# Intermediate stores moved from SyncE's DMA queue to GpSimd's, and one Sqrt taken first of all

## The chip, the cores and the metric

The kernel runs on one core of a Trainium2 chip. The metric is the time of one execution on the device in microseconds (us). Five engines work side by side, each with an instruction stream of its own that it works through in order: TensorE (PE in the profile; its weight loads are PEld), VectorE (DVE), ScalarE (ACT), GpSimd (POOL) and SyncE (SP). Transfers between device memory and on-chip memory (SBUF) are issued by an engine as an instruction of its stream; where that instruction has to wait for its data or for a free buffer, everything behind it on this engine waits too.

## The reference, cut to what matters

One layer of a hybrid block on x of 1024 tokens by 2048 features: eight heads of neighbourhood attention and eight groups of a gated long convolution (Hyena) share one input projection, their results go through one output projection, and a mixture of 16 experts follows.

```python
h = rms_norm(x, mix_norm_g[i])
proj = jnp.einsum('bsd,de->bse', h, w_in[i])
q, k, v = jnp.split(proj[..., :3 * ATTN_WIDTH], 3, axis=-1)
...
attn = neighbourhood_attention(q, k, v, rpb[i])
filters = implicit_filters(s, filt_w1[i], filt_b1[i], filt_w2[i], filt_b2[i], filt_w3[i], filt_freq[i])
hy = hyena_mixer(proj[..., 3 * ATTN_WIDTH:], conv_w[i], conv_b[i], filters, filt_bias[i])
mixed = jnp.concatenate([group_rms_norm(attn, attn_out_g[i], N_ATTN_HEADS),
                         group_rms_norm(hy, hyena_out_g[i], N_HYENA_GROUPS)], axis=-1)
x = x + jnp.einsum('bsd,de->bse', mixed, w_out[i])
x = x + expert_choice_moe(rms_norm(x, ffn_norm_g[i]), w_router[i], w_gate[i], w_up[i], w_down[i])

def hyena_mixer(u, conv_w, conv_b, filters, filt_bias):
    u = short_conv(u, conv_w, conv_b)
    z = u[..., HYENA_ORDER * HYENA_WIDTH:]
    for o in range(HYENA_ORDER):
        gate = u[..., o * HYENA_WIDTH:(o + 1) * HYENA_WIDTH]
        z = gate * bidirectional_fft_conv(z, filters[:, o, 0], filters[:, o, 1], filt_bias[o])
    return z

def bidirectional_fft_conv(u, h_fwd, h_bwd, skip):
    taps = jnp.concatenate([h_fwd, jnp.zeros_like(h_fwd[:1]), h_bwd[:0:-1]], axis=0)
    spec = jnp.fft.rfft(uf, n=n, axis=1) * jnp.fft.rfft(taps, n=n, axis=0)[None]
    y = jnp.fft.irfft(spec, n=n, axis=1)[:, :length]
    return (y + uf * skip.astype(jnp.float32)).astype(u.dtype)
```

## The kernel before, in words

Each fp32 operand of a large product is split in two parts, high and low (`split`: ACT casts, DVE subtracts), and three products of the parts are added up. The stages are:

- **Start (0 to about 103 us).** `load_h` loads x in eight tiles of 128 tokens, sums squares on ACT (`sq`), takes the root (`st`), scales (`xs`), transposes and splits. The high part `hh` stays in SBUF, the low part goes to device memory (`lo_d`). The first input projection is done beside it.
- **Filters (about 103 to 812 us).** The input projection (`pj`) runs on as a stream that loads weights (`w`) and low parts (`hl`, five buffers, 608 loads) through SP's queue. Woven into it are six attention heads and 16 calls of `filt(u, o)`. Each `filt` makes two spectra `H` (i = 0, 1; one buffer, 128 by 1026) and stores each to `Hd` (32 stores of 513 KB).
- **Hyena (about 812 to 1640 us).** Eight groups. `hyena(u)` loads two spectra (`H<-Hd`) on SP and convolves through transforms written as matmuls.
- **Closing (about 1640 to 2140 us).** The last two attention heads (6 and 7), and the output projection (`o`) as a new stream: 56 loads `s<-sd` of 1 MB on SP into two buffers, and weights `b`.
- **Routing and experts (2140 to 3293 us).** Not touched.

The output projection is done by a Strassen-like scheme with seven products. For that `store_mixed` makes, for each of eight channel blocks, seven combinations of the mixed halves, splits each in a high and a low part (`mxh`, `mxl`, one buffer each), and stores both to one of the tensors `sd1` to `sd7` (112 stores of 256 KB; in the listings below `sd_60` is sd1, `sd_61` sd2, `sd_62` sd3, `sd_63` sd4, `sd_64` sd5, `sd_65` sd6, `sd_66` sd7). What the first of two visits to a channel block needs later goes to `half` (16 stores of 256 KB). Attention heads and Hyena groups share these buffers' pattern: `mxh` can be written again only when its store has landed.

The order of the work is set by `weave`: it lets the stream and the heads or groups take turns by a running estimate of PE's time. Each engine then gets its instructions in about that order, and the builder's own scheduler may move rows that don't depend on each other. Loads, stores and weights of the first stages all stand in SP's one stream. POOL has before the experts only small memsets (`T`, `pT`, `fz`, `raw`, `z`, `Z`) and 20 loads of constants: `m`, `amask`, `at_g`, `qkg`, `hy_u`, `hy_g` and others. ACT's first operation is `sq` (L173), its first root stands in L175.

The lines of the change: L143 (`self.eps`), L588 (store of `H`), L757 (stores of `mxh` and `mxl`), L772 (stores of `mx` and `mxo` to `half`). Loads that stand behind these on SP: L280 (`hl`), L266 (`w`), L691 (`H<-Hd`), L815 (`T`, the bias table of a head), L957 (`s<-sd`), L962 (`x`).

Of the kernel before, what the change touches and what calls it, by code (L numbers as in the profile page):

```python
# [7 lines left out]
F32 = mybir.dt.float32  # L8
# [3 lines left out]
AF = mybir.ActivationFunctionType  # L12
# [5 lines left out]
P = 128  # L18
# [19 lines left out]
class Block:  # L38
# [90 lines left out]
    def build(self, ctx):  # L129
        tc, nc, a = self.tc, self.nc, self.a  # L130
        self.dram = ctx.enter_context(tc.tile_pool(name="dram", bufs=1, space=DRAM))
        cst = ctx.enter_context(tc.tile_pool(name="cst", bufs=1))
        self.sd = {i: self.dram.tile([4, P, 2, NU, P], F32, name=f"sd{i}") for i in range(1, 8)}
        self.half = self.dram.tile([NU, 2, P, 512], F32, name="half")
        self.xg = self.dram.tile([S, D + 16], F32, name="xg")
        self.lo_d = self.dram.tile([KD, P, S], F32, name="lo_d")
        self.Hd = self.dram.tile([NU, 2, P, 2, NF], F32, name="Hd")
        self.ident = cst.tile([P, P], F32, name="ident")
        nc.scalar.dma_start(self.ident, a["c_ident"])
        eps = cst.tile([P, 16], F32, name="eps")  # L140
        nc.vector.memset(eps, EPS)
        self.eps = eps[:, 0:1]
        self.aff = cst.tile([P, NT // 2, 2, NE], F32, name="aff")  # L143
        self.gate = cst.tile([P, NE], F32, name="gate")
        self.idx = cst.tile([P, NE], I32, name="idx")
        self.outer = ctx
        with ExitStack() as self.tail:
            self.phase1()
            self.phase2()
        self.phase3(ctx)  # L150
# [387 lines left out]
    def filt(self, u, o):  # L538

        nc, a, pl, L = self.nc, self.a, self.fw, self.pace("filt")  # L540
        if o == 0:
            self.win = pl.tile([P, S], F32, name="win", bufs=1)
            nc.sync.dma_start(self.win, a["c_win"][u * P:(u + 1) * P, :])
        win = self.win
        w3 = pl.tile([P, 2, P], F32, name="w3", bufs=1)
        nc.sync.dma_start(w3, a["filt_w3"][u, o])
        yield 3.0
        ws = pl.tile([P, 512], F32, name="bt", bufs=1)[:, :2 * P].rearrange("p (i c) -> p i c", i=2)
        nc.vector.tensor_tensor(ws[:, 0], w3[:, 0], w3[:, 1], op=ALU.add)
        nc.vector.tensor_tensor(ws[:, 1], w3[:, 0], w3[:, 1], op=ALU.subtract)  # L550
        wr = pl.tile([P, 2, P], R, name="wr", bufs=2)
        nc.scalar.copy(wr, ws)
        nc.vector.tensor_tensor(wr[64:], ws[64:], wr[64:].bitcast(F32), op=ALU.subtract)
        p = self.ps("F")
        self.mm(p[:, :1], w3[:64, 0], self.hid_0, True, True)
        z0 = pl.tile([P, 1], F32, name="z0", bufs=2)
        nc.vector.scalar_tensor_tensor(z0, p[:, :1], win[:, 0:1], self.hy_s[:, u, o:o + 1],
                                       op0=ALU.mult, op1=ALU.add)
        yield L["td"]
        sc = 1.0 / 1024  # L560
        for i in range(2):
            z = pl.tile([P, S + 1], F32, name="fz", bufs=1)
            nc.gpsimd.memset(z[:, S:S + 1], 0.0)
            for s in range(2):
                sl = slice(s * 512, s * 512 + 512)
                p = self.ps("F")
                self.mm(p, wr[:, i], self.hid_h[:, sl], True, False)
                self.mm(p, wr[:, i], self.hid_l[:, sl], False, True)
                nc.vector.tensor_tensor(z[:, sl], p, win[:, sl], op=ALU.mult)
                yield L["fz"]  # L570
            nc.vector.tensor_copy(z[:, 0:1], z0)
            ze, zo = self.fold_o(pl, z)
            H = pl.tile([P, NF], F32, name="H", bufs=1)
            fl = self.sin_fold(pl, zo) if i else self.cos_fold(pl, ze)
            yield L["ff"] + 1.5
            hl = self.tsplit4(pl, fl, "FT")
            yield L["td"]
            if i:
                yield from self.sin_even(pl, H, hl, sc, "F", L)
            else:  # L580
                yield from self.cos_even(pl, H, hl, ze, sc, "F", L)
            z = ze[:, 0:512] if i else zo
            hl = self.tsplit4(pl, self.halves(z[:, 0::2]) + self.halves(z[:, 1::2]), "FT")
            yield L["td"]
            self.odd(pl, H, hl, sc, "F", i)
            if i == 0:
                nc.vector.tensor_scalar(H[:, 0:257:256], H[:, 0:257:256], 0.5, None, op0=ALU.mult)
            nc.sync.dma_start(self.Hd[u, o, :, i], H)  # L588
            yield L["dd"]
        yield L["fe"]  # L590

# [149 lines left out]
    def store_mixed(self, pool, u, src, g, role, L):  # L741

        nc = self.nc
        v, head = u % NU, u < NU
        second = head != (v < self.EARLY)
        m, p = [], []  # L750

        def store(i, x):
            hi = pool.tile([P, 512], R, name="mxh", bufs=1)
            lo = pool.tile([P, 512], R, name="mxl", bufs=1)
            self.split(hi, lo, x)
            for j, t in enumerate((hi, lo)):
                nc.sync.dma_start(self.sd[i][:, :, j, v, :].rearrange("t p c -> p t c"),  # L757
                                  t.bitcast(F32).rearrange("p (t c) -> p t c", t=4))

        for h in range(2):  # L760
            if second:
                p.append(pool.tile([P, 512], F32, name="mxp", bufs=2))
                nc.sync.dma_start(p[h], self.half[v, h])
            o = pool.tile([P, 4, P], F32, name="mxo", bufs=1)
            self.norm4(pool, o, src(h))
            yield L["mx"]
            pt = self.ps(role)
            self.flip(pt, [o[:, i] for i in range(4)])
            m.append(o.rearrange("p i c -> p (i c)") if h else pool.tile([P, 512], F32, name="mx", bufs=1))
            nc.scalar.activation(m[h], pt, AF.Copy, scale=g)  # L770
            if not second:
                nc.sync.dma_start(self.half[v, h], m[h])  # L772
            if h == 0 or not head:
                store((1 if head else 2) if h == 0 else 4, m[h])
            if h == 0:
                yield L["tt"]
        tt = nc.vector.tensor_tensor
        if second:
            yield L["tt"]
            tt(p[1], m[1], p[1], op=ALU.add)  # L780
            store(5, p[1])
        if head:
            yield L["tt"]
            tt(m[1], m[0], m[1], op=ALU.subtract)
            store(7, m[1])
        if second:
            yield L["tt"]
            a0, y0 = (m[0], p[0]) if head else (p[0], m[0])
            tt(a0, p[1], a0, op=ALU.subtract)
            store(6, a0)  # L790
            yield L["tt"]
            tt(y0, y0, a0, op=ALU.subtract)
            store(3, y0)
        self.mixed.add(u)
# [627 lines left out]
```

## Time and profile before

| what | value |
|---|---|
| median of 3 runs | 3293.3 us (3292.95 to 3294.88) |
| profiled execution: time, span | 3295.26 us, 3293.5 us |
| PE, DVE, ACT, POOL busy | 96%, 74%, 56%, 3% of the span |
| mean granted TensorE clock | 0.985 |
| SP's queue (q1), GpSimd's queue (q0) | 837.26 MB, 36.49 MB |
| chain that ended last | PE 83%, DMA 9%, DVE 3%, issue 3%, ACT 1% |

The span is the time from the first to the last instruction of the profiled execution; 1.8 us of the execution lie outside it. The chain that ended last is followed back from the last instruction, at each step to what released it. PE holds 83% of it, so a change off PE can only win where PE stands still or runs at its lower clock.

### The profile page before, as it was taken

The page shows a single profiled execution, that of the slowest core. Times are in us where ns is not written, and L with a number is a line of the kernel's source. Part 1 is how long each engine was busy: PE and PEld are TensorE (multiplying, and loading weights), DVE is VectorE, ACT ScalarE, POOL GpSimd, SP SyncE. Part 2 cuts the span into 40 slices and gives each one's busy share as a digit, 9 for nine tenths or more (in the row PEclk, how much of TensorE's full clock was granted, in tenths as well). Part 3 has the DMA queues.
Part 4 walks back from the last instruction along what each step waited for, and adds up shares of the span by engine and source line. Part 5 has one row for each costly group of instructions (what it writes and reads, how often), then busy time and mean ns, then how long its engine had stood idle before and what let it go on. Part 6 is the DMA issues. An engine that isn't in the chain of part 4 may idle for free.

```text
span 3293.5 us, 47095 instructions
## 1 busy us (share of the span) xinstructions
PE 3164.4 (96%) x17040; PEld 2756.7 (84%) x17040; DVE 2432.1 (74%) x3648; ACT 1851.8 (56%) x2881; POOL 85.1 (3%) x200
## 2 busy tenths in 40 slices
PE   8999999999999999999997999949999999999998
PEld 8899999998888888889986777738888888888887
DVE  5677776764567777677677455589989999899997
ACT  5455555543334344344353222548888888888886
POOL 0000000000000000000000000000000000000000
PEclk9999999999999999999998999979999999999999
DMA  7555555556676666665467886698999999999993
GB/s 250 192 166 171 178 188 191 166 180 207 198 223 203 202 218 210 223 208 193 156 224 253 288 282 209 224 365 343 403 398 391 405 404 404 392 398 405 403 404 133
DMA packets 311913, 876.82 MB, mean 266 GB/s; under 512 B 27108, under 2 KB 127631, under 8 KB 247936
## 3 DMA queue, kind: packets, MB, share of 16 engines
q1 hardware_dynamic: 305888, 837.26, 69.7%
q0 software_dynamic: 5648, 36.49, 4.3%
q8 instruction: 134, 2.20, 0.3%
q14 instruction: 99, 0.81, 0.1%
q10 hardware_dynamic: 144, 0.07, 0.0%
HBM read 781.07 MB, written 92.37 MB: 265 GB/s over the span
## 4 chain that ended last, share of the span: by engine, by line
PE 83%; DMA 9%; DVE 3%; issue 3%; ACT 1%; SPq 0%; POOLq 0%; POOL 0%; DVEq 0%; ACTq 0%
PE pa L68 30%; PE pj L68 29%; PE o L68 6%; PE c L68 5%; PE f L68 4%; DMA s<-sd 3%; PE a L68 3%; PE ct L79 2%; PE tp L1333 1%; DMA hl<-lo_d 1%; DMA sd<-mxl 1%; PE a L79 1%; PE ft L79 1%; DMA w<-in_w_down_dram 1%; PE t L79 1%
## 5 line engine op out<-in xcount | busy, mean ns | idle before, releaser
L60 ACT CAST wh<-w 128x1024 fp32r<-128x1024 f32 (+2 forms) x1180 | 990.2, 846 | 593.2 <-PE pj L68 369.8
L61 DVE TENSOR_TENSOR wl<-w,wh 128x1024 fp32r<-128x1024 f32 (+2 forms) x1180 | 1122.5, 966 | 243.4 <-ACT wh L60 183.7
L68 PE MATMUL pa<-wh,xh 128*128 128x512 f32 x1024 | 400.3, 391 | 0.0
L68 PE MATMUL pa<-wh,xl 128*128 128x512 f32 x1024 | 398.6, 389 | 0.0
L68 PE MATMUL o<-wh,s 128*128 128x512 f32 x896 | 305.3, 409 | 25.5 <-DMA s<-sd 24.3
L68 PE MATMUL pj<-wh,hh 128*128 128x384 f32 x896 | 315.0, 352 | 2.9 <-ACT wh L60 2.9
L68 PE MATMUL pa<-wl,xh 128*128 128x512 f32 x1024 | 315.3, 389 | 0.0
L68 PE MATMUL pj<-hh,wh 128*128 128x512 f32 x768 | 314.8, 410 | 0.0
L68 PE MATMUL pj<-hl,wh 128*128 128x512 f32 x768 | 305.6, 398 | 7.0 <-DMA hl<-lo_d 6.7
L68 PE MATMUL pj<-wl,hh 128*128 128x384 f32 x896 | 304.7, 340 | 0.0
L68 PE MATMUL pj<-wh,hl 128*128 128x384 f32 x896 | 304.0, 339 | 0.0
L68 PE MATMUL pj<-hh,wl 128*128 128x512 f32 x768 | 303.1, 395 | 0.0
L68 PE MATMUL pa<-wh,el 128*128 128x512 f32 x1024 | 282.2, 397 | 0.2 <-DVE el L61 0.2
L68 PEld LDWEIGHTS o<-wh,s 128*128 128x128 f32 x896 | 172.4, 193 | 68.9 <-DMA s<-sd 32.8
L68 PEld LDWEIGHTS pa<-wl,xh 128*128 128x128 f32 x1024 | 192.2, 188 | 40.3
L68 PEld LDWEIGHTS pa<-wh,xh 128*128 128x128 f32 x1024 | 192.4, 188 | 39.4
L68 PEld LDWEIGHTS pa<-wh,xl 128*128 128x128 f32 x1024 | 192.3, 188 | 39.4
L68 PEld LDWEIGHTS pa<-wh,el 128*128 128x128 f32 x1024 | 187.2, 189 | 36.0 <-DVE el L61 0.7
L68 PE MATMUL o<-wl,s 128*128 128x512 f32 x448 | 180.0, 402 | 0.0
L68 PEld LDWEIGHTS pj<-wh,hh 128*128 128x128 f32 x896 | 169.3, 189 | 8.8 <-ACT wh L60 3.2
L68 PEld LDWEIGHTS pj<-hh,wl 128*128 128x128 f32 x768 | 144.7, 188 | 34.4
L68 PEld LDWEIGHTS pj<-wl,hh 128*128 128x128 f32 x896 | 169.6, 189 | 2.5 <-DVE wl L61 1.2
(331 smaller groups left out, 5543.2 us busy)
## 6 DMA issues: line engine op xcount, KB each, us to landing
hl<-lo_d SPq DMA_DIRECT2D x608, 256.0 KB, 3.1
w<-in_w_down_dram SPq DMA_DIRECT2D x128, 1024.0 KB, 11.8
w<-in_w_up_dram SPq DMA_DIRECT2D x127, 1024.0 KB, 10.4
w<-in_w_gate_dram SPq DMA_DIRECT2D x127, 1024.0 KB, 10.5
s<-sd SPq DMA_DIRECT2D x56, 1024.0 KB, 6.5
w<-in_w_at_dram SPq DMA_DIRECT2D x120, 384.0 KB, 3.4
w<-in_w_hy_dram SPq DMA_DIRECT2D x96, 256.0 KB, 3.6
Hd<-H SPq DMA_DIRECT2D x32, 513.0 KB, 4.3
```

Of the source, the lines that this page charges most:

```text
L60: nc.scalar.copy(hi, src)
L61: nc.vector.tensor_tensor(lo, src, hi.bitcast(F32), op=ALU.subtract)
L68: self.nc.tensor.matmul(out, w, x, start=start, stop=stop)
L79: self.nc.tensor.transpose(pt[:, i * P:(i + 1) * P], b, self.ident)
L1333: self.nc.tensor.transpose(pt[:, i * P:(i + 1) * P], src[:, c:c + (P - 1) * step + 1:step], self.ident)
```

## The change: what it does

1. A constant's root is taken on ACT right after the constant `eps` is set, into a tile of one column that nobody reads.
2. The 32 stores of `H` go out by GpSimd's queue.
3. The 112 stores of `mxh` and `mxl` and the 16 stores to `half` go out by GpSimd's queue.

```diff
@@ -140,6 +140,8 @@
         eps = cst.tile([P, 16], F32, name="eps")
         nc.vector.memset(eps, EPS)
         self.eps = eps[:, 0:1]
+        warm = cst.tile([P, 1], F32, name="warm")
+        nc.scalar.activation(warm, self.eps, AF.Sqrt)
         self.aff = cst.tile([P, NT // 2, 2, NE], F32, name="aff")
@@ -585,7 +587,7 @@
                 nc.vector.tensor_scalar(H[:, 0:257:256], H[:, 0:257:256], 0.5, None, op0=ALU.mult)
-            nc.sync.dma_start(self.Hd[u, o, :, i], H)
+            nc.gpsimd.dma_start(self.Hd[u, o, :, i], H)
             yield L["dd"]
@@ -754,7 +756,7 @@
             for j, t in enumerate((hi, lo)):
-                nc.sync.dma_start(self.sd[i][:, :, j, v, :].rearrange("t p c -> p t c"),
+                nc.gpsimd.dma_start(self.sd[i][:, :, j, v, :].rearrange("t p c -> p t c"),
                                   t.bitcast(F32).rearrange("p (t c) -> p t c", t=4))
@@ -769,7 +771,7 @@
             if not second:
-                nc.sync.dma_start(self.half[v, h], m[h])
+                nc.gpsimd.dma_start(self.half[v, h], m[h])
```

On ACT, at the start of the program, before:

```order
L139 DMA ident<-in_c_ident_dram 128x128
L173 ACT_TABLE_LOAD
L173 ACTIVATE sq_105,st_104<-x_101 128x1024
L173 ACTIVATE sq_107,st_104<-x_101 128x1024
L174 ACTIVATE st_104<-st_104,eps 128x1
L175 ACT_TABLE_LOAD
L175 ACTIVATE st_104<-st_104 128x1
```

and after (lines are two higher from here on):

```order
L139 DMA ident<-in_c_ident_dram 128x128
L144 ACT_TABLE_LOAD
L144 ACTIVATE warm<-eps 128x1
L175 ACTIVATE sq_107,st_106<-x_103 128x1024
L175 ACTIVATE sq_109,st_106<-x_103 128x1024
L176 ACTIVATE st_106<-st_106,eps 128x1
L177 ACTIVATE st_106<-st_106 128x1
```

The table load between the squares and the root is gone; one stands ahead of the first root now.

On POOL, at the change from filters to Hyena, before the last rows of the filter stage are memsets; after:

```order
L759 DMA sd_66<-mxh 128x4x128
L759 DMA sd_66<-mxl 128x4x128
L590 DMA Hd<-H 128x1026
L399 DMA hy_u<-in_hy_u_dram 128x96
L401 DMA hy_g<-in_hyena_out_g_dram 128x8
L707 MEMSET z 128x1
```

The two loads of Hyena's constants stand behind the last store of a spectrum on the same engine. At the change from Hyena to closing it is alike; on POOL after:

```order
L774 DMA half<-mxo 128x512
L759 DMA sd_63<-mxh 128x4x128
L759 DMA sd_63<-mxl 128x4x128
L806 DMA amask<-in_c_mask_dram 128x64
L808 DMA at_g<-in_attn_out_g_dram 128x8
L810 DMA qkg<-in_qk_g_dram 128x2
L837 MEMSET T 64x64
```

The loads of the last heads' constants stand behind the last two stores of the last group. On SP, in the closing stage around the first loads of `sd_60`, before:

```order
L1071 DMA w_22405<-in_w_up_dram 128x2048
L757 DMA sd_60<-mxh 128x4x128
L757 DMA sd_60<-mxl 128x4x128
L1071 DMA w_22407<-in_w_gate_dram 128x2048
L957 DMA s<-sd_60 128x2048
L757 DMA sd_64<-mxh 128x4x128
L757 DMA sd_64<-mxl 128x4x128
L957 DMA s<-sd_60 128x2048
L757 DMA sd_66<-mxh 128x4x128
L757 DMA sd_66<-mxl 128x4x128
L757 DMA sd_65<-mxh 128x4x128
L757 DMA sd_65<-mxl 128x4x128
```

and after:

```order
L1073 DMA w_22407<-in_w_up_dram 128x2048
L1073 DMA w_22409<-in_w_gate_dram 128x2048
L959 DMA s<-sd_60 128x2048 x3
L1111 DMA out_dram<-x_19142 128x512
L959 DMA s<-sd_60 128x2048
```

The four loads of `sd_60` follow one another, and the ten stores that stood among them are on POOL.

## Rows read from the trace of the kernel before

**Rows 1.** Busy time by stretch: us, length, busy (instructions) by engine, clock, DMA.
```profile
165.00:785.00 620.00, 618.30 (x4034) 587.98 (x4033) 428.62 (x1000) 338.71 (x691) 9.59 (x66) 1.00 0.55 176
785.00:850.00 65.00, 60.08 (x276) 47.66 (x276) 26.24 (x52) 18.85 (x38) 1.51 (x7) 0.97 0.76 248
850.00:1650.00 800.00, 797.54 (x4633) 702.38 (x4632) 556.83 (x978) 318.81 (x693) 7.36 (x60) 1.00 0.63 202
1700.00:1800.00 100.00, 79.00 (x412) 65.12 (x410) 79.90 (x122) 47.51 (x75) 1.09 (x6) 0.91 0.77 276
1800.00:1900.00 100.00, 88.97 (x411) 71.03 (x412) 42.45 (x60) 26.92 (x44) 1.06 (x2) 0.94 0.84 290
```

**Rows 2.** Waits of SP's queue: line, waited for, us in total, times, longest.
```profile
SPq L757 <- ACT mxh L60: 62.2, 35, 7.5
...
SPq L588 <- DVE H L536: 42.4, 26, 7.8
```

**Rows 3.** Waits of all engines: ACT for the store of mxh.
```profile
ACT mxh L60 <- DMA sd<-mxh: 51.7, 22, 8.1
```

**Rows 4.** Chain of waits at the start: begin, length, what.
```profile
8.41 1.28 ACT L175
```

**Rows 5.** Chain of waits in the Hyena stage, 1049 to 1075.
```profile
1068.69 0.37 SPq L757
...
1069.16 4.95 DMA hl<-lo_d
```

**Rows 6.** Waits of PE, 850 to 1650.
```profile
PE pj L68 <- DMA hl<-lo_d: 1.8, 2, 0.9
```

**Rows 7.** Chain of waits in the closing stage, 1735 to 1830.
```profile
1747.38 7.48 DMA s<-sd
...
1815.77 5.63 DMA s<-sd
```

**Rows 8.** PE's instructions there; in brackets the idle time before them.
```profile
1742.13 0.39 PE L68 MATMUL o<-wh,s 128*128 128x512 f32 x1
...
1754.91 0.79 PE L68 MATMUL o<-wh,s 128*128 128x512 f32 x1 [3.16 <-DMA s<-sd]
...
1804.32 0.79 PE L68 MATMUL o<-wh,s 128*128 128x512 f32 x1 [5.58 <-DMA s<-sd]
...
1821.44 0.50 PE L68 MATMUL o<-wh,s 128*128 128x512 f32 x1 [4.01 <-DMA s<-sd]
```

**Rows 9.** PE by stretch behind two stalls: us, length, busy, clock, DMA.
```profile
1754.90:1760.00 5.10, 5.09 (x13) 0.50 0.96 339
...
1821.40:1826.00 4.60, 4.56 (x13) 0.63 1.06 341
```

**Rows 10.** DMA issues: line engine op xcount, KB each, median us to landing.
```profile
Hd<-H SPq DMA_DIRECT2D x32, 513.0 KB, 4.3
...
sd<-mxh SPq DMA_DIRECT2D x56, 256.0 KB, 3.4
...
m<-in_c_dft_dram POOLq DMA_DIRECT2D x5, 258.0 KB, 4.7
```

**Rows 11.** POOL's DMA instructions: shapes, xcount, busy us, mean ns.
```profile
L1206 POOL DMA_INDIRECT xg<-xg,idx x16 | 30.2, 1886 | 391.2 <-DMA w<-in_w_down_dram 377.8 <-PE pa L68 9.1 <-ACT wh L60 4.3
...
L378 POOL DMA_DIRECT2D m<-in_c_dft_dram x5 | 3.0, 598 | 2.7 <-DVE ml L61 1.8 <-POOLq L1412 0.9
```

**Rows 12.** SP's queue at the change from filters to Hyena.
```profile
806.93 0.38 SPq L588 DMA_DIRECT2D Hd<-H  x1
...
812.76 0.32 SPq L691 DMA_DIRECT2D H<-Hd  x1
```

**Rows 13.** Chain of waits at the change from Hyena to closing.
```profile
1649.37 6.43 DMA T<-in_rpb_t_dram
```

**Rows 14.** SP's queue, closing stage, 1786 to 1820.
```profile
1806.60 0.36 SPq L757 DMA_DIRECT2D sd<-mxl  x1
1814.47 0.36 SPq L757 DMA_DIRECT2D sd<-mxh  x1
```

## The prediction

> **What bounds the kernel now.** I read the busy time by stretch first, because all three edits touch the stages before the experts and PE is the engine with the most work. PE is busy for 618.30 of 620 us in the filter stage and for 797.54 of 800 in the Hyena stage; it lacks 4.9 us of 65 at the change between them, and 21.0 and 11.0 us of 100 in two stretches of the closing stage [rows 1]. So a store that no longer holds up SP is worth little in the two long stages, at most 1.7 and 2.5 us, and the gain has to come from the start, the change of stages and above all the closing. Next I read what SP's queue waits for. Its stores of `mxh` wait 62.2 us for ACT and its stores of `H` 42.4 us for DVE [rows 2]; while they wait, every load behind them waits too. But SP's wait is a loss only where a load then comes late to PE. Therefore I looked in the chain of waits for loads that were issued right behind a store, and then at PE's idle time before the instruction that reads the load.
>
> **The change, part by part.**
>
> *The root at the start.* The chain holds 1.28 us of ACT at L175 between the sums of squares and the root [rows 4]; by the order of instructions that is a table load, and afterwards it stands before x has arrived, where ACT is idle. All of it is on the chain that starts PE. Behind it the first product needs also its weights and a second tile of x, so not all of the 1.28 arrives: I take -1.0, bounds -1.3 and 0. Late next are the weights. One table load more stands later, between two exponentials of the closing stage; by the same row it costs 1.3 us on ACT, which is busy for 47.5 of 100 us there [rows 1], so nothing, and 1.3 if PE waits for that exponential.
>
> *A store on POOL instead of SP.* What the instruction costs POOL: 598 ns for a direct load of `m` with 128 pieces, 1886 ns for an indirect one [rows 11]. The 112 stores of `mxh` and `mxl` have 512 pieces of 512 bytes, which no row shows on POOL; 0.6 to 1.9 us each, and I take 1.0, between the two. 160 stores make 160 us of an engine that is busy 7 to 10 us in each long stage [rows 1], so POOL's own time is hidden; its memsets may stand behind a store that waits for DVE. What the landing costs: 4.7 us for 258 KB by POOL against 3.4 for 256 KB by SP [rows 10], so +1.3 us for each store, bounds 0 and +3 (the price of the indirect issue over the direct one, 1.3, on top, rounded up).
>
> *Filter stage.* The 32 spectra leave SP. PE has 1.7 us to win; -0.5, bounds -1.0 and +1 (a spectrum that lands later keeps the only buffer of `H` longer, but no wait of ACT for a store of `H` is among the waits).
>
> *Change of stages, 785 to 850.* Hyena's first load `H<-Hd` is issued at 812.76, 5.8 us behind the last store of a spectrum at 806.93 [rows 12], since it waits for that landing. By POOL it lands 1.3 us later, and the constants `hy_u` now stand behind the store on the same engine. Against that, loads `hl` no longer stand behind stores. +0.5, bounds -3 and +4.
>
> *Hyena stage.* The pattern is a store of `mxl` issued at 1068.69 and the load `hl` only behind it, at 1069.16, 4.95 us on the chain [rows 5]; PE waits 0.9 us for it. There are two such waits, 1.8 us in all [rows 6]. They go: -1.8. Against that ACT has already waited 22 times, 51.7 us, for a store of `mxh` to land [rows 3]; 1.3 us more at each is 29 us on an engine that is busy 319 of 800 us, mostly hidden, +0.5. Sum -1.3, bounds -2.5 and +3.
>
> *Change to closing.* The bias table `T` is loaded at 1649.37 and its landing, 6.43 us, is on the chain [rows 13]. The constants that are added to it now stand on POOL behind the last stores of the last group, and `T` itself waits for the landing of such stores. +1.5, bounds 0 and +4.
>
> *Closing, 1751.* SP issues the load `s` at 1747.38, right behind a pair of stores; it takes 7.48 us [rows 7], and PE stands still for 3.16 us before it works on at 1754.91 [rows 8]. PE ended the tile that this buffer held before with the product at 1742.13 [rows 8], and then worked on the other buffer; so without the stores the load can go out about 1743, some 4.5 us sooner, and PE doesn't wait. Behind that stall PE runs at a granted clock of 0.50, that is 1.2 instead of 2.4 GHz, for 5.10 us [rows 9]; at the higher level this work takes half, 2.5 us less. Together -5.7. VectorE is busy 79.90 of these 100 us [rows 1] and would become the bound for part of it, so I take seven tenths, -4.0, bounds -5.7 and 0.
>
> *Closing, 1798 to 1821.* PE's wait of 5.58 us until 1804.32 [rows 8] is for the first load of `sd_60`, which needs the stores of just before; 1.3 us more landing makes it longer: +1.3. Then SP stands from 1806.60 to 1814.47 waiting for `mxh` [rows 14], and only behind three stores does the load go out at 1815.77 [rows 7]; PE idles 4.01 us before 1821.44 [rows 8]. PE had two loaded tiles to work on between 1804.32 and 1817.4, so the first buffer was free at half of that, about 1811. Now the four loads follow one another, the load goes out at 1811 and lands at 1811 + 5.63 = 1816.6, before PE needs it. That is -4.0, and 4.60 us at a clock of 0.63 behind it [rows 9] at the full clock would be 2.9: -1.7. With +1.3, sum -4.4, bounds -6 and +2.
>
> Sum: -1.0 - 0.5 + 0.5 - 1.3 + 1.5 - 4.0 - 4.4 = -9.2 us. The profiled execution took 3295.3, so 3286.1; it lies 2.0 above the median of the runs shown, so against that 3284.1.
>
> **A rule against it.** VectorE is busy in 74% of the span, and still POOL's direct loads took 598 ns on the mean [rows 11], no sign of a block. The Trainium skill, "SBUF — State Buffer", section "SBUF: two separate sides", says that descriptors of a transfer issued by GpSimd are written by its own cores and stand still while VectorE holds the shared port in its two-port modes; it gives about 620 ns alone and 3100 ns beside such a copy. The 598 ns agree with its undisturbed figure; an estimate by its other one would add 2.5 us to each store's landing. What such a delay does to this kernel is the second rival.
>
> **The rivals.**
>
> *Hidden anyway.* The stalls in the closing only change their names: DVE and ACT make the products' terms in one chain with single buffers, and PE waits for that chain instead of for a load. For it: DVE's 79.90 of 100 us [rows 1], and the later landing that lengthens this chain. Against it: both stalls [rows 8] end with a load whose buffer was free before. Then 1.0 of the start and a quarter of the closing's 8.4 remain: about -3, 3290.
> The Trainium skill, "DMA: Bandwidth & Descriptors", section "Issuing engines are not separate DMA queues", states that issuing from another engine only saves the time on the sequencer that issues. By that rule alone this rival would be the outcome; the row of SP waiting for `mxh` from 1806.60 to 1814.47 [rows 14] speaks against it, since what is saved there is a wait, not an issue.
>
> *Stores land too late.* Mechanism: `mxh` and `mxl` have one buffer each, and each stage change waits for the last store. If a landing by POOL takes not 1.3 but 4 us more, the 22 waits of ACT [rows 3] grow by 88 us; at the place where stores follow one another in the closing (three landings one behind the other before 1815) that is +12, at `T` and at `H<-Hd` +4 each: +20, against the forecast's -9.2 without its own +1.3, +1.5 and +0.5, that is -12.5. Result +8, 3301. It decides from about +2.5 us on, where 5 times the extra landing passes 12.5. For it: 512 pieces per store, which no row shows by POOL. Against it: 4.7 us for `m` [rows 10].
>
> *The change doesn't free the queue:* the loads would wait for the stores' landing all the same, because `s` and `H<-Hd` read what was stored. True for the first of each tensor only; the order of the loads of `sd_60` shows three that wait for nothing new. Result within 1 us of before, 3292.
>
> **How the numbers follow.** Chances: forecast 0.58, hidden 0.24, late stores 0.11, not freed 0.07. The forecast's own range is -15 to -3 (all lower bounds at once would be -19.5, all upper ones +14). A measurement of this kernel can tell about 0.2%, 6.6 us, from no change, that is 3286.7 to 3299.9. The forecast passes 3286.7 in three of four cases, 0.44, the hidden case in one of five, 0.05: faster 0.49. Slower is most of the late case, 0.07, and a little of the rest, 0.02: 0.09. Same 0.42. For 8 in 10: from 3276 to 3298.
>
> **What would show it.** Right: the table load of 1.28 us before 2 us and the first product about 1 us sooner; no stall of 3 us in the closing that ends with a load `s` issued right behind stores, and the clock at 1.0 where it was 0.50; stores by POOL that land in 4 to 6 us. Wrong: a median landing of these stores over 6 us, more than 100 us of ACT's wait for `mxh`, PE waiting for `T` or `H<-Hd` over 3 us longer than before, or the closing stretch as long as before with waits for `mxo` or `mxp` in place of `s`.

## The result: 1.5% slower, and the profile after

The changed kernel takes 3343.2 us (median of 4 runs, 3335.1 to 3349.5) against 3293.7 before (4 runs, 3293.0 to 3294.9): 1.0149 times as long, 95% interval 1.0122 to 1.0175. The forecast was 3284 with a range of 3276 to 3298. It was wrong in sign and far outside the range. All medians and ratios in this document leave out two executions of about three times the length, one of `after_b2c` (9888.65 us) and one of the kernel before on the chip of the first four experiments (9751.85 us).

Busy time by stretch of the changed kernel, columns as in [rows 1]; the stages lie a little later in it:

```profile
165.00:785.00 620.00, 611.58 (x3987) 581.36 (x3986) 423.87 (x991) 335.32 (x683) 46.19 (x125) 1.00 0.53 173
785.00:850.00 65.00, 57.72 (x270) 46.78 (x269) 24.31 (x50) 19.16 (x40) 6.80 (x15) 0.95 0.70 234
850.00:1650.00 800.00, 780.65 (x4476) 681.63 (x4475) 544.42 (x954) 307.97 (x672) 55.06 (x123) 0.99 0.60 197
...
1800.00:1900.00 100.00, 76.59 (x380) 63.69 (x380) 51.66 (x85) 32.86 (x56) 9.21 (x15) 0.86 0.60 206
...
2250.00:3220.00 970.00, 969.75 (x4428) 805.55 (x4427) 886.10 (x794) 798.27 (x865) 50.17 (x28) 1.00 1.00 394
```

The Hyena stage was at 797.54 of 800 us [rows 1] and has now lost 16.9 us of PE's work in the same length, the filter stage 6.7. From 2250 on PE is as full as it was. To see where the lag grows I took the n-th product of the same operands in both traces and subtracted the starts: the changed kernel is 5.7 us late where the kernel before stood at 785, 8.6 at 850, 31.4 at 1486, 52.7 at 2191, and 53.0 at the end. So 5.7 us are lost up to the end of the filter stage, 2.9 at the change, 22.8 in the Hyena stage and 21.3 in the closing. Two kernels below whose instructions up to 785 are those of before differ from it there by -1.7 and -0.7 us, so one profile tells a stage to about 2 us at best. The four runs of the changed kernel lie 14 us apart, and the profile is of one of the two long ones; in which stage they part can't be told, so a lag of a kernel with stores on POOL may be off by several us more.

What PE waits for between 850 and 1650 in the changed kernel (total, times, longest):

```profile
PE c L68 <- DVE tlo L61: 8.7, 6, 2.4
PE ct L79 <- DVE Y L605: 8.6, 4, 3.2
...
PE pj L68 <- DMA hl<-lo_d: 0.2, 1, 0.2
```

The wait for `hl`, 1.8 us before [rows 6], has gone as forecast. In its place PE waits 17.3 us for two products of VectorE, which is the whole 16.9 that it lost. The lag grew by 22.8 because PE also runs slower behind three of these waits (2.95, 2.09 and 3.23 us): its granted clock was 0.50 there, 1.2 instead of 2.4 GHz, for 10.2 us in all, where the kernel before ran this whole stage at 1.00. At half the clock that costs another 5.1 us. Behind the second stall shown below, columns as in [rows 1]:

```profile
1084.00:1086.00 2.00, 2.00 (x8) 1.71 (x7) 1.55 (x4) 1.28 (x3) 0.00 (x0) 0.50 0.24 76
```

VectorE was late with these two products because of what stood ahead of them in its stream. Its instructions around the first of these stalls, in brackets the idle time before each:

```profile
1075.52 0.69 DVE L61 TENSOR_TENSOR mxl<-mxp,mxh 128x512 fp32r<-128x512 f32 x1 [5.12 <-DMA sd<-mxl]
1076.12 1.22 DVE L602 TENSOR_TENSOR Y<-Z,H 128x1028 f32<-128x1028 f32 x1
1077.27 0.68 DVE L61 TENSOR_TENSOR tlo<-ct,thi 128x512 fp32r<-128x512 f32 x1
...
1081.18 0.69 DVE L61 TENSOR_TENSOR mxl<-mx,mxh 128x512 fp32r<-128x512 f32 x1 [2.10 <-DMA sd<-mxl]
...
1082.73 0.69 DVE L605 TENSOR_TENSOR Y<-Z 128x514 f32<-128x514 f32 x1
```

and PE's instructions there:

```profile
1078.00 0.51 PE L68 MATMUL c<-mh,tlo 128*128 128x256 f32 x2 [2.41 <-DVE tlo L61]
1083.57 1.09 PE L79 MATMUL ct<-ident,Y 128*128 128x128 f32 x4 [2.95 <-DVE Y L605]
```

The write to `mxl` waits 5.12 us until the store of the last `mxl` has landed, since there is one buffer; `Y` and `tlo` stand behind it, and PE waits for both. The stores themselves, on POOL:

```profile
1069.10 0.76 POOL L759 DMA_DIRECT2D sd<-mxh  x1 [4.99 <-ACT mxh L60]
1069.87 0.75 POOL L759 DMA_DIRECT2D sd<-mxl  x1
1074.44 0.75 POOL L759 DMA_DIRECT2D sd<-mxh  x1 [3.81 <-ACT Z L527]
1076.61 0.75 POOL L759 DMA_DIRECT2D sd<-mxl  x1 [1.42 <-DVE mxl L61]
```

The `mxl` written at 1075.52 for 0.69 us, until 1076.21, is issued at 1076.61, 0.40 us later. In the kernel before, the chain has

```profile
1067.97 0.70 DVE mxl L61
```

until 1068.67, and then the issue at 1068.69 [rows 5], 0.02 us later. The landing, in medians (KB, us to landing), answers to [rows 10]:

```profile
Hd<-H POOLq DMA_DIRECT2D x32, 513.0 KB, 4.9
...
sd<-mxh POOLq DMA_DIRECT2D x56, 256.0 KB, 3.9
sd<-mxl POOLq DMA_DIRECT2D x56, 256.0 KB, 4.6
```

3.9 against 3.4 us for `mxh`, and 0.4 us later issued: a buffer is free about 0.9 us later, for `mxl` (3.5 us before) about 1.5. The waits over the whole run, answering to [rows 3]:

```profile
ACT mxh L60 <- DMA sd<-mxh: 63.9, 22, 8.4
...
DVE mxl L61 <- DMA sd<-mxl: 50.2, 20, 5.1
```

ACT's 51.7 us have become 63.9. DVE's line in the kernel before was

```profile
DVE mxl L61 <- DMA sd<-mxl: 33.0, 12, 8.0
```

so that the two wait 29.4 us longer together. Between 850 and 1650 alone, before:

```profile
ACT mxh L60 <- DMA sd<-mxh: 34.0, 18, 3.5
DVE mxl L61 <- DMA sd<-mxl: 19.9, 9, 4.2
```

and after 38.3 us (17 times) for ACT and 37.7 (16 times) for DVE: 22.1 us more, 17.8 of them on DVE.

The filter stage loses at another place. No write to `mxh` or `mxl` waits for a store there. DVE overwrites `mxo` in place and has to wait until the store of `mxo` to `half` has landed, 9.5 us in all where it was 2.5, and three of PE's four longest waits in this stage, 5.2 us together, begin behind such a write. The longest of the three, on DVE and on PE:

```profile
549.84 0.69 DVE L786 TENSOR_TENSOR mxo<-mx,mxo 128x512 f32<-128x512 f32 x1 [3.54 <-DMA half<-mxo]
550.45 0.68 DVE L61 TENSOR_TENSOR tlo<-ft,thi 128x512 fp32r<-128x512 f32 x1
...
551.19 0.80 PE L68 MATMUL f<-mh,tlo 128*128 128x258 f32 x2 [2.31 <-DVE tlo L61]
```

### The profile page after: what moved, and what is told of

Read it like the earlier page. It is cut to its first block, busy times and chain, and to the rows that moved or that the text cites. A ratio compares the mean times of both kernels' runs of the same rounds, so it can differ in the third digit from the quotient of the medians.

```text
span 3346.3 us, 47118 instructions
## 1 busy us (share of the span) xinstructions
PE 3173.8 (95%) x17040; PEld 2761.7 (83%) x17040; DVE 2431.7 (73%) x3648; ACT 1852.5 (55%) x2883; POOL 196.0 (6%) x360
## 2 busy tenths in 40 slices
DMA packets 260713, 876.82 MB, mean 262 GB/s; under 512 B 27108, under 2 KB 70287, under 8 KB 196736
## 4 chain that ended last, share of the span: by engine, by line
PE 75%; issue 11%; DMA 8%; DVE 4%; POOL 1%; ACT 1%; SPq 0%; POOLq 0%; ACTq 0%; DVEq 0%
PE pa L68 29%; PE pj L68 23%; PE o L68 6%; PE c L68 4%; PE f L68 4%; PE a L68 3%; DMA s<-sd 2%; DMA sd<-mxl 1%; PE tp L1335 1%; PE ct L79 1%; POOL sd L759 1%; PE a L79 1%; PE ft L79 1%; PE l L68 1%; DMA hl<-lo_d 1%
## 6 DMA issues: line engine op xcount, KB each, us to landing
w<-in_w_up_dram SPq DMA_DIRECT2D x127, 1024.0 KB, 10.6
```

## The experiments

Each median is of 4 to 11 runs; each ratio is to the kernel before on the same chip, whose median there is 3293.7 to 3295.9 us, with a 95% interval. "Lag" is the growth of PE's lag, as above, up to the end of the filter stage (785), in the Hyena stage (850 to 1486) and in the closing (1486 to 2191), from one profile each.

| kernel | median, us | ratio, interval | lag: filter, Hyena, closing |
|---|---|---|---|
| the change | 3343.2 | 1.0149 (1.0122 to 1.0175) | 5.7, 22.8, 21.3 |
| `warm_only` | 3295.9 | 0.9995 (0.9985 to 1.0005) | -3.0, 0.4, -2.0 |
| `hd_only` | 3297.1 | 1.0007 (0.9997 to 1.0017) | 2.0, -0.4, -1.8 |
| `mix_only` | 3339.8 | 1.0135 (1.0118 to 1.0152) | 6.6, 25.2, 10.6 |
| `after_b2` | 3310.6 | 1.0049 (1.0033 to 1.0066) | 7.3, -2.8, 9.2 |
| `mix_oldorder` | 3339.2 | 1.0132 (1.0117 to 1.0148) | 2.0, 19.1, 24.0 |
| `sp_neworder` | 3322.7 | 1.0081 (1.0067 to 1.0095) | 5.1, 9.1, 16.3 |
| `sp_twice` | 3349.8 | 1.0165 (1.0152 to 1.0178) | 6.5, 25.9, 18.3 |
| `close_only` | 3317.2 | 1.0060 (1.0046 to 1.0075) | -1.7, -1.3, 22.9 |
| `after_b2c` | 3306.5 | 1.0026 (1.0013 to 1.0039) | 7.1, -3.2, 7.0 |
| `before_b2` | 3291.5 | 0.9989 (0.9980 to 0.9998) | -0.7, -2.5, -3.3 |
| `warm_b2` | 3291.0 | 0.9984 (0.9973 to 0.9995) | -1.0, -4.6, -0.1 |
| `hyena_pool_b2` | 3290.9 | 0.9983 (0.9971 to 0.9995) | -1.5, -2.8, 0.1 |
| `warm_b2c` | 3294.8 | 0.9998 (0.9988 to 1.0008) | 0.5, -3.9, 1.2 |

**Which part does it.** Each of the three parts alone: `warm_only` has the two lines at `self.eps`, `hd_only` the one at `Hd`, `mix_only` the two in `store_mixed`.

> Part 1 alone: the early Sqrt, all stores on SyncE's queue. In the changed kernel the PE's projection is 0.8 us ahead at 15 us and 1.96 us ahead at 46 us, so if that is the table load alone: 3293.7 - 1.5 = 3292 (3291 to 3293.5). Rival (the lead came from the other parts): no change, 3293.7.

> Part 2 alone: the 32 spectra go out by GpSimd's queue. Theory A (the loss is the single mxh and mxl buffers waiting for a later landing): the spectra cost almost nothing, 3293 to 3296, PE's waits in the filter stage as before. Theory B (GpSimd's in-order stream: stores and memsets hold each other up): the filter stage's 7.7 us come back, 3299 to 3303. Both: up to 3 us at the change from filters to Hyena.

> Part 3 alone: the 112 stores of mxh and mxl and the 16 of half by GpSimd's queue. Theory A: nearly the whole loss, 3335 to 3348, with about 23 us in the Hyena stage and about 20 in the closing. Theory B: part 3 alone loses less than the whole by the filter stage's 7.7 us and by what stands behind stores of spectra, 3325 to 3335.

The early root and the spectra can't be told from no change; part 3 is the loss. Its time is in the range that theory A gave, but its closing lost 10.6 us where about 20 were expected, and 21.3 in the whole change; parts 1 and 2 give no reason for that, and it was not traced to a cause. The early root does what was said, as ACT's first rows in the changed kernel show:

```profile
1.19 1.28 ACT L144 ACT_TABLE_LOAD   x1 [1.19 <-PEq L1414]
2.48 0.20 ACT L144 ACTIVATE warm<-eps 128x1 f32<-128x1 f32 x1
...
8.32 0.29 ACT L177 ACTIVATE st<-st 128x1 f32<-128x1 f32 x1
```

The root stands at 8.32 where it was behind a load of 1.28 us that began at 8.41 [rows 4]. PE's first product of `fh` and `hh` starts at 14.13 against 14.90. But the lag of PE at 46 us is not its mark: three kernels without the early root are 1.5 to 2.6 us ahead there too.

**Is it the buffer?** Two buffers for `mxh` and `mxl` in the Hyena stage, on top of the whole change:

```diff
-            hi = pool.tile([P, 512], R, name="mxh", bufs=1)
-            lo = pool.tile([P, 512], R, name="mxl", bufs=1)
+            hi = pool.tile([P, 512], R, name="mxh", bufs=2 if getattr(self, "hw", None) is pool else 1)
+            lo = pool.tile([P, 512], R, name="mxl", bufs=2 if getattr(self, "hw", None) is pool else 1)
```

> The changed kernel with two buffers each for mxh and mxl in the Hyena stage (not elsewhere, where they don't fit). Theory A (a single buffer makes ACT and DVE wait for the landing, and what PE needs stands behind them): the Hyena stage's 23 us come back nearly whole, 3315 to 3325. Theory C (it is the new order of DVE's and ACT's instructions, or the stores' time on GpSimd, and not the landing): less than 8 us come back, 3335 to 3345.

```profile
165.00:785.00 620.00, 613.44 (x4004) 583.07 (x4003) 425.31 (x994) 335.23 (x683) 46.36 (x124) 1.00 0.55 174
850.00:1650.00 800.00, 798.26 (x4641) 703.26 (x4640) 557.78 (x979) 316.44 (x690) 56.68 (x126) 1.00 0.63 203
```

In these rows by stretch the Hyena stage is back at 798.26 us of PE, more than before, with the stores still on POOL; the filter stage, where the buffers are single, keeps its loss. ACT and DVE still wait for landings in the Hyena stage, 20.4 and 16.1 us, but PE waits only 1.6. The scheduler also moved some rows of ACT and DVE with the buffers; no run holds their order with two buffers. That the closing also lost 12 us less, with single buffers there, I did not expect; it was not traced to a cause, and `mix_only`, with single buffers everywhere, lost only 10.6 there.

**Landing or order?** The builder's scheduler had also moved the splits into `mxh` and `mxl` on ACT and DVE in front of `Z` and `Y` in some groups. The first stall shown above is such a place. In the kernel before, the same `mxl`, the 21st, stands behind `Y` and `Z` and waits 0.43 us where it waited 5.12 in the changed kernel:

```profile
1061.74 1.23 DVE L601 TENSOR_TENSOR Z<-Z,H 128x1028 f32<-128x1028 f32 x1
1063.39 0.69 DVE L61 TENSOR_TENSOR mxl<-mxp,mxh 128x512 fp32r<-128x512 f32 x1 [0.43 <-DMA sd<-mxl]
```

Three kernels hold every instruction of PE, ACT and DVE in a given order by order-only edges, from a table of the order that another kernel has:

```diff
...
+            if last is not None:
+                tc.add_manual_dep(i, last, kind, reason="keep_order")
+            last = i.name
...
         Block(tc, args).run()
+        keep_order(tc, nc)
```

`mix_oldorder` is part 3 in the order of before, `sp_neworder` the kernel before in the order of part 3; the third, `sp_twice`, comes further down.

> Part 3 alone (stores of mxh, mxl and half by GpSimd's queue), with PE's, ACT's and DVE's instructions held in exactly the order of the kernel before. Landing theory (a store by GpSimd lands later, and single buffers make ACT and DVE wait for it): the loss of part 3 alone stays, 3330 to 3345. Order theory (the scheduler took the stores on the empty GpSimd stream for early and moved the splits into mxh and mxl ahead of what PE needs): the loss goes, 3294 to 3302. In between: both.

> The stores stay on SyncE's queue as before, but PE's, ACT's and DVE's instructions stand in exactly the order that part 3 gave them. Landing theory: as before, 3293 to 3300. Order theory: slow like part 3 alone, 3325 to 3345.

By stretch, `mix_oldorder`:

```profile
165.00:785.00 620.00, 615.75 (x4019) 585.79 (x4018) 427.67 (x996) 337.44 (x688) 30.82 (x98) 1.00 0.55 175
850.00:1650.00 800.00, 784.26 (x4520) 685.23 (x4519) 546.04 (x959) 306.96 (x673) 54.90 (x123) 1.00 0.61 197
```

and `sp_neworder`:

```profile
165.00:785.00 620.00, 613.82 (x3995) 583.34 (x3994) 424.59 (x992) 335.30 (x685) 9.54 (x66) 1.00 0.55 173
850.00:1650.00 800.00, 792.02 (x4572) 694.70 (x4570) 552.76 (x968) 311.18 (x677) 7.30 (x60) 1.00 0.64 200
```

In the old order the whole loss of part 3 stays: the queue alone is enough, in the Hyena stage (19.1 us) and in the closing (24.0). At the place of the first stall `mxl` waits 2.35 us there. But the landing theory's other half fell: the new order alone, with stores on SP, costs 0.8%, where that theory expected next to nothing and its rival a little more. It carries most of the filter stage's part (613.82 us there, against 615.75 with the old order and 618.30 before; the waits of `mxo` for `half` are 7.8 us with the new order alone and 3.9 with the old). The two don't add up (0.8% and 1.3%, together 1.35%); that each takes up the same slack is my reading, which no run shows.

**Later, without GpSimd.** `sp_twice` keeps the order and SP's queue and stores each buffer a second time, to a scratch tensor:

```diff
+                nc.sync.dma_start(self.sx[i][:, :, j, v, :].rearrange("t p c -> p t c"),
+                                  t.bitcast(F32).rearrange("p (t c) -> p t c", t=4))
```

> The kernel before, PE's, ACT's and DVE's instructions in exactly its order, but SyncE's queue stores each mxh and mxl twice: to its place and to a scratch tensor that nobody reads. GpSimd's queue is not used. A buffer is then free one issue (0.37 us) and some transfer time later, about as much later as by GpSimd's queue (there 0.37 us from the write to the issue and 0.4 to 1.3 us of landing). Landing theory: it loses like part 3 alone in the old order, 3315 to 3340. Rival (the loss belongs to GpSimd's stream, not to the time until the buffer is free): 3294 to 3303.

```profile
850.00:1650.00 800.00, 777.65 (x4451) 675.29 (x4451) 540.45 (x946) 307.33 (x671) 5.87 (x58) 1.00 0.69 218
```

and its waits over the whole run:

```profile
ACT mxh L60 <- DMA sx<-mxh: 68.8, 21, 9.4
DVE mxl L61 <- DMA sx<-mxl: 68.3, 23, 9.5
```

Here the second store lands 4.15 us behind the write of `mxh` and 5.05 behind that of `mxl` (medians of those whose landing the trace tells); by POOL in the changed kernel the only store lands after 4.29 and 5.01, in the kernel before after 3.46 and 3.63. So the buffers come free about as late as in the change, without GpSimd, and the kernel loses more than `mix_oldorder` and 10 us beyond the range I gave. Some of it is the second stores' own traffic and SP's longer stream (PE's wait for `hl` in this stretch is 3.6 us); no run separates these. What it shows is that the loss doesn't need GpSimd: this kernel has little slack for a later free buffer, whoever issues the store.

**The closing.** Stores on POOL in the closing alone; then a second buffer there too, for which the buffers of `x2` go from 8 to 6.

```diff
-                nc.sync.dma_start(self.sd[i][:, :, j, v, :].rearrange("t p c -> p t c"),
+                (nc.gpsimd if self.closing else nc.sync).dma_start(self.sd[i][:, :, j, v, :].rearrange("t p c -> p t c"),
```

> Stores by GpSimd's queue only in the closing stage. By the forecast's terms for the closing (two loads of s no longer behind stores, T later): -4.0 - 4.4 + 1.5 = -6.9, 3288. By the closing of part 3 alone, where 1486 to 2191 lost 10.5 us although no load of s waits behind a store any more: 3302 to 3308.

> The changed kernel with two buffers each for mxh and mxl in the Hyena stage and in the closing (room for it by six instead of eight buffers of x). Landing theory: of the closing's 21 us all but the 6 to 7 that PE waits for the load of g behind GpSimd's last stores come back, so against two buffers in the Hyena stage alone (3310.6) some 3 to 10 us less, 3300 to 3307. Rival (in the closing it is g and the new order, not the buffers): 3309 to 3313.

The closing by itself loses 0.6%, more than either number I had given. PE's instructions in the changed kernel, answering to [rows 8], idle time before them in brackets:

```profile
1769.04 1.11 PE L79 MATMUL t<-ident,pe 128*128 128x128 f32 x4 [4.36 <-ACT pe L857]
...
1781.00 0.40 PE L68 MATMUL a<-qkh,qkh 128*128 128x288 f32 x1 [2.78 <-ACT qkh L740]
...
1788.69 0.80 PE L68 MATMUL o<-wl,s 128*128 128x512 f32 x1 [5.67 <-DVE wl L61]
...
1799.95 0.47 PE L68 MATMUL o<-wh,s 128*128 128x512 f32 x1
...
1848.06 0.79 PE L68 MATMUL o<-wh,s 128*128 128x512 f32 x1 [6.38 <-DMA s<-sd]
...
1861.48 0.50 PE L68 MATMUL o<-wh,s 128*128 128x512 f32 x1 [0.74 <-DMA s<-sd]
...
1876.88 1.94 PE L79 MATMUL t<-ident,xg 128*128 128x128 f32 x8 [6.24 <-DVE xg L1114]
```

The two stalls that I counted on are gone: the product that waited 3.16 us now starts at 1799.95 and waits for nothing, and the one that waited 4.01 waits 0.74 (at 1861.48). The third, for the first load of `sd_60`, went from 5.58 to 6.38. In their place PE waits for ACT and DVE, whose splits into `mxh` and `mxl` now stand ahead of `pe`, `qkh` and `wl` and wait for a store. On ACT and on DVE, ahead of the first and the third row above:

```profile
1766.24 0.62 ACT L60 CAST mxh<-mxo 128x512 fp32r<-128x512 f32 x1 [6.44 <-DMA sd<-mxh]
...
1768.17 0.72 ACT L857 ACTIVATE pe<-pe,ast 128x512 f32<-128x512 f32 x1
...
1786.21 0.69 DVE L61 TENSOR_TENSOR mxl<-mxp,mxh 128x512 fp32r<-128x512 f32 x1 [4.71 <-DMA sd<-mxl]
...
1787.42 2.35 DVE L61 TENSOR_TENSOR wl<-b,wh 128x1024 fp32r<-128x1024 f32 x2
```

PE's last row, at 1876.88, is new and has another cause; in the chain:

```profile
1864.69 0.73 POOL sd L759
1865.42 10.53 DMA g<-in_ffn_norm_g_dram
...
1876.04 0.70 DVE xg L1114
```

The weight `g` of the next stage was always issued by POOL. In the kernel before it was issued at 1802.8, landed in 10.0 us and was first used at 1829.4. It now stands behind the last store, is issued at 1865.4, and VectorE waits until it lands 10.53 us later. With two buffers in the closing as well, 6.3 us of this wait stay, and of the 49 us of the change 8.5 are left (0.26%): the filter stage's 7, and `g`. The intervals of `after_b2` and `after_b2c` just overlap, so the second buffer's share of the closing is probable, not settled.

**A better version?** Two buffers in the Hyena stage without the change, with the early root, and with the Hyena stores alone on POOL:

> The kernel before with two buffers each for mxh and mxl in the Hyena stage, stores on SyncE's queue. If ACT's and DVE's waits for landings are hidden in the kernel before, as I took them to be: 3291 to 3295, at best the two waits of PE for hl (1.8 us) go.

> The early Sqrt and two buffers each for mxh and mxl in the Hyena stage, all stores on SyncE's queue. If GpSimd's queue is worth nothing beside the second buffer: 3288 to 3292, no slower than with the Hyena stores on GpSimd's queue. If the queue is worth its 1.8 us in the Hyena stage: 2 to 3 us slower than that.

> The early Sqrt, and in the Hyena stage alone stores by GpSimd's queue with two buffers each for mxh and mxl; the heads' stores and the spectra stay on SyncE's queue. From the changed kernel with two buffers the Hyena stage gains 2.8 us between 850 and 1486, and the early Sqrt some 1.5: 3289 to 3292. Rival (the change of queue at the start of the closing costs what the stage wins): 3293 to 3296.

> The early Sqrt and two buffers each for mxh and mxl in the Hyena stage and in the closing, six buffers of x, all stores on SyncE's queue. If landings bound the closing before too (three one behind the other before PE's stall of 4 us): 3282 to 3289. If not, as with two buffers in the Hyena stage alone: 3289 to 3293.

The first three are 0.11 to 0.17% faster than the kernel before, each interval below 1, and can't be told from one another. With the buffer there, GpSimd's queue is worth nothing that these runs measure: 0.9984 without it, 0.9983 with it. A second buffer in the closing at the price of two of `x2` gives nothing.

## Why the prediction was wrong, point by point

- **The root at the start** (-1.0): right in the trace, 0.77 us at PE's first product. In the time it is below what 11 runs tell.
- **A store on POOL.** 0.75 us on POOL against the 1.0 that I took; a buffer free 0.9 to 1.5 us later against 1.3. Both sizes lie within the bounds that I gave.
- **Hyena stage** (-1.3): this is the step that failed. I had written that ACT's 22 waits would grow by 29 us, "mostly hidden, +0.5". The 22 waits are of the whole run; 18 of them, 34.0 us, lie in this stage. There ACT's grew by 4.3 us and DVE's, which I had not counted, by 17.8. They were not hidden: 17.3 us of PE's waits follow, and 5.1 us at half the clock behind them, of 22.8 us lost. I judged by ACT's busy share, 319 of 800 us [rows 1]. A busy share says nothing about what stands behind a wait in an in-order stream: one wait holds back `tlo` and `Y` behind it. By the trace of the kernel before, PE takes a `tlo` 3.4 us after it is written in the median of this stage, but within 1 us in 6 of 126 cases, and a wait of up to 5.1 us outlasts that. The bound of +3 came from the same mistake.
- **Filter stage** (-0.5): the spectra cost nothing that can be told, as said. I left out that the heads' stores lie in this stage too. The one to `half` holds back the write of `mxo` in place, and the new order costs most of it; 5 to 7 us.
- **Change of stages** (+0.5, up to +4): 2.9. **Change to closing** (+1.5): the load of `T` waited for a landing as said; the lag grew by 1.2 us between 1486 and 1711.
- **Closing** (-8.4): both loads of `s` came in time and both stalls went. But the same step failed as in the Hyena stage: ACT and DVE wait for single buffers, and PE behind them, far more than for three tenths of one stall; 21.3 us were lost where 8.4 were to be won. And I looked at which POOL loads stand behind the stores at two places, and not at the third, `g`: 6.2 us.
- **The rivals.** "Stores land too late" named the mechanism, single buffers, but put its threshold at 2.5 us of extra landing, with the stage changes and the closing as its places. It put nothing down for ACT's 88 us more of waiting. Here it decided at about 1 us, in the Hyena stage and in the closing. "Hidden anyway" was right on the closing's stalls. The rule of the Trainium skill's "DMA: Bandwidth & Descriptors", section "Issuing engines are not separate DMA queues", that another issuing engine saves only sequencer time, fits `hyena_pool_b2` against `warm_b2`: nothing to gain. The block by VectorE's copies that the Trainium skill's "SBUF — State Buffer", section "SBUF: two separate sides", warns of did not appear: the POOL rows above last 0.76 us with VectorE at work (1069.10) and 0.75 with VectorE idle (1074.44). VectorE's rows there are TENSOR_TENSOR and not copies, so what a copy would do no run here shows.

## What to carry to other kernels

Before a store moves to another queue, ask when its buffer is free again, not when the issuing engine is: with one buffer, as here, a landing that is 1 us later can hold back every stream that writes the buffer, and what stands behind that write. A busy share doesn't tell slack; look at how long PE has waited, or nearly waited, for what stands behind the waiting instruction. And list everything that the new queue already carries, up to the stage after.

## What was not expected of the hardware

A store of 512 pieces of 512 bytes takes POOL 0.75 us and one of `H` 0.55, each within 0.03 us. POOL begins such a store 0.40 us after its data is written, where SP began 0.03 after it (medians of 56 stores each). The run as a whole moved the same 876.82 MB in 260,713 packets where it was 311,913.
